# One late modulation sum per scan step, six among the intra-chunk matrices and four in the second branch

## The chip, the cores and the metric

The kernel runs on one core of a Trainium2 chip. A core has a matrix engine (TensorE, PE in the profile), a vector engine (VectorE, DVE), a scalar engine (ScalarE, ACT), a general engine (GpSimd, POOL) and a synchronising engine (SyncE, SP), which here issues the transfers between the chip's memory and the core's. Each engine runs its own instructions in order and waits on semaphores for the others. The metric is the time of one execution of the whole program in microseconds of the device, as a median of runs.

## What is computed

One layer of a hybrid backbone over 512 latent tokens (width 1024) and 256 context tokens: a modulated norm, one wide input projection, two mixers, a gated sum, an output projection, a second modulated norm and an MLP.

```
sh1, sc1, gt1, sh2, sc2, gt2 = split(silu(c) @ w_ada + b_ada, 6)
h  = rms_norm(x, g_norm1) * (1 + sc1) + sh1                  # hc likewise, for the context
aq, ak, av, dq, dk, dv, dz, da, db, ga, gd = split_cols(h @ w_in)
y_attn = window_ctx_attention(rope(norm(q)), rope(norm(k)), v, context k and v, sink)
o_d    = gated delta rule in both directions (chunks of 64), context state first, then latent
y = sigmoid(ga) * (y_attn @ w_br_attn) + sigmoid(gd) * ((rms_norm(o_d) * silu(dz)) @ w_br_dn)
x = x + gt1 * (y @ w_out)
x = x + gt2 * (relu(modulate(x, sh2, sc2) @ w_mlp1) ** 2 @ w_mlp2)
```

In the delta rule each chunk needs a triangular inverse, the matrix `intra = decay * (q k^T)` and, over the chunks, a scan that carries the state:

```
u = uv - w @ S;   o = q_dec @ S + intra @ u;   S = exp(g_last) * S + k_tail^T @ u
```

Of the modulation vector, the first two parts (`sh1`, `sc1`) are needed at the start. The other four (`gt1`, `sh2`, `sc2`, `gt2`) are needed only after the mixers; in this kernel they are the "late" part.

## The kernel before

The kernel is written in a tile framework: the program says what to compute and which buffers to use, and a scheduler orders the instructions of each engine by their dependences and their place in the program. So where a call stands in the code decides roughly, but not exactly, where its instructions run.

Activations lie transposed, with channels on the 128 partitions and the 512 tokens along the row. Every large product is a 128x512 matmul in three parts (high times high, high times low, low times high, `mm3`, L313 to L315), since each operand is split into a high and a low part: ScalarE copies the high part (L259 for weights, L184 for activations) and VectorE subtracts it for the low part (L262, L185). Weights come through a ring of four raw buffers of 512 KB (`wr`, L250) and two split ones (`wh`, `wl`).

**The fill.** Between the small matmuls of the delta rule (32 to 64 rows) PE runs large products of other work: the first branch's projection (`br_a`, 96 products) and the gate tiles (`gate_tiles`, 24 products for each tile, L1004, then an activation that L148 issues). `run_fill(n)` takes the next `n` of these 432 products. The table `FILL` says how many go where: 144 in the context scan, `FILL[1]` for each of the two `combine` calls, `FILL[2]` for each of the two intra-chunk calls, and three numbers (8, 7, 3) for the three phases of each latent scan step. What is left then runs after the scan. `combine` multiplies the halves of the inverse in two bursts of small matmuls (L854/L855 and L864/L865); between them ScalarE evicts the first result (L856) and `CPAUSE` products run.

**The intra-chunk matrices.** For each of two groups, `half_products` computes q k^T in two halves (L754), VectorE multiplies by the decay (L1245, L1246), and then for each of two halves of the partitions ScalarE copies blocks (L1252 twice, L1253, L1254), 32x512 each.

**The scan.** A step of `chain_step` runs for both directions in three phases: L1119 (state times key and query), VectorE's L1123 and L1124 (decay and difference), L1131 (times the inverse), L1137 and ScalarE's L1141 and L1143, then L1152/L1156 (state and output), L1168 (new state) and L1175 or L1178/L1180 (output). The last three set off the next step.

**The late sums.** `late_mod` computes the late modulation on VectorE. Each of the 32 sums loads 512 KB of `w_ada` into a slot of the same ring (`wa`, tag `wr`) and runs one instruction of 128x1024 with an accumulator (L1070); after each eighth, L1073 adds the bias. `run_late(n)` runs the next `n`, up to 24; the last eight run in the MLP's first part. Before, two of the three phases of each latent scan step take one (16 in all), and the output projection takes the other eight.

**After the scan.** The norm of the scan's output (L1178 to L1182, table loads on ScalarE, L1285), transposes on PE (L1290), the last gate tiles, then the second branch: eight tiles of 12 products (L1312's `mm3`), each evicted by L1314, added by L1316 and split by L184/L185 into `Y`. The output projection (`residual`, L1336) reads all eight `Y`.

Of the kernel before, what the change touches and what calls it, by code (L numbers as in the profile page):

```python
# [11 lines left out]
AF = mybir.ActivationFunctionType  # L12
# [3 lines left out]

NU = 167
NWR, NWS = 4, 2
FILL = 144, 28, 36, (8, 7, 3)
INV = 2, 12, 18, 0  # L20
QTS = 7, 5, 4, 7, 3, 6, 10, 7
CO = 1
# [4 lines left out]
WARM = 3, 6, 4, 4  # L27
NONES = 16
AHEAD = 2
LATE = 1  # L30
HPAUSE = 2
FPAUSE, CPAUSE = 12, 12
NPL = ()
WEARLY = 0
ND1 = 3
# [10 lines left out]
HC = CH // 2  # L46
# [53 lines left out]
def tile_layer(ctx: ExitStack, tc: tile.TileContext, I: dict, out: bass.AP, dbg=None):  # L100
# [995 lines left out]
    eGs = const.tile([P, 2, NM], F32, name="eGs")  # L1096
    for r in range(2):
        A.activation(eGs[64 * r:64 * r + 64], eG[64 * (1 - r):64 * (1 - r) + 64], AF.Copy)
    oss = small([P, NCL, 4], "oss", bufs=1)
    hv = lambda ap: ap.rearrange("p (q v) -> p q v", q=4)  # L1100
    state = [None, None]
# [134 lines left out]
    for g in range(2):  # L1236
        ms = slice(16 * g, 16 * g + 16)
        es = slice(512 * g, 512 * g + 512)
        run_fill(FILL[2] - FPAUSE)
        qq_ = bank(2)  # L1240
        qD, qO = diag_off(qq_)
        for _ in half_products(qq_, 1 + g, qT):
            run_fill(FPAUSE)
        for d in range(2):
            V.tensor_tensor(ia[d][:, ms, :HC], v3(ED[d][:, es]), qD, op=ALU.mult)  # L1245
        V.tensor_tensor(v3(EO[:, es]), v3(EO[:, es]), qO, op=ALU.mult)  # L1246
        qq_.free()
        eo = v3(EO[:, es])
        for a in range(2):
            lo, hi = quad(a, 0), quad(a, 1)  # L1250
            for d in range(2):
                A.activation(ia[d][hi, ms, HC:], ia[d][hi, ms, :HC], AF.Copy)  # L1252
            A.activation(ia[0][lo, ms, HC:], eo[lo], AF.Copy)  # L1253
            A.activation(ia[1][hi, ms, :HC], eo[hi], AF.Copy)  # L1254
            G.memset(ia[0][hi, ms, :HC], 0.0)
            G.memset(ia[1][lo, ms, HC:], 0.0)
# [6 lines left out]
    ot = ot_.ap.rearrange("p (c q v) -> p c q v", c=NCL, q=4)  # L1263
    for n, _ in enumerate(steps(range(NCC, NC_))):
        run_fill(FILL[3][n % 3])
        if n % 3:
            run_late(LATE)
    for _ in fill:
        pass
    for b in kT + qT + KTM[1:] + VTM[1:] + XA[1] + IA + zb + Sb[0] + Sb[1]:  # L1270
# [37 lines left out]
    Y = [alloc(1024) for _ in range(8)]  # L1308
    for ct in range(8):
        w = wnext()  # L1310
        pd = bank()
        mm3(pd.ap, w, [(r32(b[:, :512]), r32(b[:, 512:])) for b in yd])  # L1312
        g = gdt[ct].ap
        V.scalar_tensor_tensor(g, g, 1.0, pd.ap, op0=ALU.add, op1=ALU.mult)  # L1314
        pd.free()
        V.tensor_tensor(g, g, gat[ct].ap, op=ALU.add)  # L1316
        split(g, Y[ct][:, :512], Y[ct][:, 512:])
# [235 lines left out]
```

## Time and profile before

| | |
|---|---|
| runs | 928.25 us median of three (928.17 to 930.97) |
| profiled execution | 923.26 us, its span 921.5 us |
| granted TensorE clock, mean | 0.996 |
| PE busy | 886.7 us (96%) |
| DVE busy | 596.6 us (65%) |
| ACT busy | 447.6 us (49%) |
| late sums (L1070) | 32, 38.9 us of VectorE |
| intra-chunk stage, 360 to 401 us | PE busy 36.89 of 41.00 us |
| latent scan, 401 to 474 us | PE busy 68.46 of 73.00 us |

A row of a group names the line, the engine, the operation, what it writes and reads, the count, the busy time, the mean of one in nanoseconds, and the idle time before it with its releaser. A row of a wait names the line that waited and the one that released it. A row of the timeline has the start and the duration in microseconds, and in brackets the idle time before.

### The profile page before, as it was taken

To read this page: it belongs to the slowest core of one execution; us is meant where nothing else is said; L and a number is where in the kernel's file an instruction comes from. 1 tells how busy PE (TensorE), PEld (TensorE's weight loads), DVE (VectorE), ACT (ScalarE), POOL (GpSimd) and SP (SyncE) were. 2 spreads that over 40 slices of the span, in tenths; PEclk is the share of its full clock that TensorE was granted. 3 is DMA by queue.
4 is the path that set the end of the run, shared out by engine and by line. 5 is a ranking of instruction groups with operands and counts; after the bars stand their busy time and mean duration, and the time that the engine had idled before them with its cause. 6 is when DMAs were issued, how large, how long until landed. Compare 5 with 4: busy or idle time off the path is not lost.

```text
span 921.5 us, 16859 instructions
## 1 busy us (share of the span) xinstructions
PE 886.7 (96%) x7082; PEld 709.2 (77%) x7082; DVE 596.6 (65%) x1021; ACT 447.6 (49%) x829; POOL 12.0 (1%) x26
## 2 busy tenths in 40 slices
PE   8999998999899999989999999999999999999998
PEld 5668767867677687767778889888888888888886
DVE  3588899997687898358865977961554235324511
ACT  5577653257568787475554434560353025213400
POOL 0000000000000002000000000000000000000000
PEclk9999999999999999999999999999999999999999
DMA  9650112110000232236424673660443224322111
GB/s 355 255 197 1 47 47 68 50 49 19 24 13 23 58 109 78 92 109 189 142 81 149 193 245 114 212 243 23 160 137 115 69 69 138 100 69 83 46 46 46
DMA packets 28443, 98.24 MB, mean 107 GB/s; under 512 B 3536, under 2 KB 4176, under 8 KB 27344
## 3 DMA queue, kind: packets, MB, share of 16 engines
q1 hardware_dynamic: 28368, 97.18, 33.0%
q8 instruction: 55, 0.90, 0.4%
q14 instruction: 20, 0.16, 0.1%
HBM read 95.07 MB, written 2.10 MB: 105 GB/s over the span
## 4 chain that ended last, share of the span: by engine, by line
PE 45%; DVE 3%; DMA 3%; ACT 1%; issue 1%; ACTq 0%
PE banks L313 14%; PE banks L314 14%; PE banks L315 14%; PE banks L1004 3%; DMA wa<-in_wada 2%; DVE m L1070 1%; DVE wl L262 1%; DMA wr<-in_wm 0%; ACT wh L259 0%; DVE m L1168 0%; ACT m L1166 0%; PE banks L1131 0%; PE banks L1290 0%; PE banks L1156 0%; ACT m L148 0%
## 5 line engine op out<-in xcount | busy, mean ns | idle before, releaser
L313 PE MATMUL banks<-m,m 128*128 128x512 f32 (+1 forms) x600 | 223.4, 377 | 2.8 <-DVE m L620 1.9
L314 PE MATMUL banks<-m,m 128*128 128x512 f32 (+1 forms) x600 | 224.5, 376 | 0.1
L315 PE MATMUL banks<-m,m 128*128 128x512 f32 (+1 forms) x600 | 224.4, 376 | 0.0
L259 ACT ACTIVATE m<-wr 128x1024 fp32r<-128x1024 f32 x68 | 72.1, 1060 | 157.0 <-PE banks L314 79.7
L313 PEld LDWEIGHTS banks<-m,m 128*128 128x128 f32 x600 | 111.8, 188 | 25.6 <-ACT m L319 2.5
L314 PEld LDWEIGHTS banks<-m,m 128*128 128x128 f32 x600 | 112.5, 188 | 22.2 <-DVE m L320 1.5
L315 PEld LDWEIGHTS banks<-m,m 128*128 128x128 f32 x600 | 112.5, 188 | 21.4 <-issue 1.2
L262 DVE TENSOR_TENSOR m<-wr,m 128x1024 fp32r<-128x1024 f32 x68 | 83.1, 1224 | 69.9 <-PE banks L314 34.2
L1004 PE MATMUL banks<-m,wh 128*128 128x512 f32 x320 | 104.1, 402 | 2.6 <-ACT m L148 2.5
L313 PE MATMUL banks<-m,wh 128*128 128x512 f32 (+1 forms) x280 | 104.0, 372 | 2.5 <-DVE m L595 1.0
L315 PE MATMUL banks<-m,wl 128*128 128x512 f32 (+1 forms) x280 | 101.6, 365 | 3.4 <-DVE wl L262 3.4
L314 PE MATMUL banks<-m,wh 128*128 128x512 f32 (+1 forms) x280 | 102.4, 366 | 0.0
L1437 DVE SCALAR_TENSOR_TENSOR m<-banks,modT,m 128x512 f32<-128x512 f32 x32 | 24.0, 750 | 101.0 <-PE banks L315 101.0
L262 DVE TENSOR_TENSOR wl<-wr,wh 128x1024 fp32r<-128x1024 f32 (+1 forms) x58 | 62.1, 1071 | 29.7 <-ACT wh L259 29.3
L259 ACT ACTIVATE wh<-wr 128x1024 fp32r<-128x1024 f32 (+1 forms) x58 | 54.5, 940 | 40.1 <-PE banks L314 17.8
L1004 PEld LDWEIGHTS banks<-m,wh 128*128 128x128 f32 x320 | 59.1, 188 | 15.6 <-ACT m L148 2.9
L1004 PE MATMUL banks<-m,wl 128*128 128x512 f32 x160 | 65.4, 409 | 0.0
L315 PEld LDWEIGHTS banks<-m,wl 128*128 128x128 f32 x280 | 53.3, 192 | 11.9 <-DVE wl L262 4.0
L313 PEld LDWEIGHTS banks<-m,wh 128*128 128x128 f32 x280 | 53.5, 191 | 11.2 <-DVE m L595 1.3
L184 ACT ACTIVATE m<-m 128x512 fp32r<-128x512 f32 (+1 forms) x56 | 35.2, 631 | 54.9 <-DVE m L1420 21.5
L314 PEld LDWEIGHTS banks<-m,wh 128*128 128x128 f32 x280 | 53.4, 191 | 8.1 <-issue 1.0
L185 DVE TENSOR_TENSOR m<-m,m 128x512 fp32r<-128x512 f32 (+1 forms) x56 | 38.3, 688 | 18.8 <-ACT m L184 18.3
(237 smaller groups left out, 1266.5 us busy)
## 6 DMA issues: line engine op xcount, KB each, us to landing
wr<-in_wm SPq DMA_DIRECT2D x64, 512.0 KB, 3.6
wr<-in_win SPq DMA_DIRECT2D x38, 512.0 KB, 3.6
wa<-in_wada SPq DMA_DIRECT2D x32, 512.0 KB, 3.9
m<-in_wada SPq DMA_DIRECT2D x8, 1024.0 KB, 12.2
m<-in_xT SPq DMA_DIRECT2D x8, 512.0 KB, 5.8
wr<-in_wbr SPq DMA_DIRECT2D x16, 256.0 KB, 2.6
wr<-in_wout SPq DMA_DIRECT2D x8, 512.0 KB, 4.5
out<-m SPq DMA_DIRECT2D x8, 256.0 KB, 2.0
```

The lines of the kernel that those rows point to most:

```text
L184: A.activation(r32(hi), src, AF.Copy)
L185: (eng or V).tensor_tensor(r32(lo), src, hi, op=ALU.subtract)
L259: h = A.activation(r32(hi), raw, AF.Copy)
L262: V.tensor_tensor(r32(lo), raw, hi, op=ALU.subtract)
L313: PE.matmul(acc, w[0][:, k, :], xhi, start=(start and i == 0), stop=False)
L314: PE.matmul(acc, w[0][:, k, :], xlo, start=False, stop=False)
L315: PE.matmul(acc, w[1][:, k, :], xhi, start=False, stop=(stop and i == n - 1))
L1004: PE.matmul(acc.ap, w[x][:, k, :], hx[k][y], start=(k == p == 0), stop=(k == KT - 1 and p == 2))
L1070: V.scalar_tensor_tensor(t.ap, wa, 0.5, scr.ap, op0=ALU.mult, op1=ALU.mult, accum_out=modT[:, grp, j:j + 1])
L1437: V.scalar_tensor_tensor(xn_[ct], acc.ap, modT[:, 3, ct:ct + 1], xn_[ct], op0=ALU.mult, op1=ALU.add)
```

## The change

Five places differ. (1) `FILL[1]` goes from 28 to 36 and `CPAUSE` from 12 to 16: each `combine` has 20 and 16 products where it had 16 and 12. (2) A new `run_both` runs fill products and after each twelfth (`LATE`) one late sum; the intra-chunk groups use it, so that 72 products take six sums. (3) A scan step takes one late sum, in its last phase, where it took two. (4) Every second tile of the second branch takes one, four in all; the output projection's `run_late(2)` finds six left. (5) The eight copies of L1252 go from ScalarE to VectorE (`tensor_copy`).

```diff
-FILL = 144, 28, 36, (8, 7, 3)
+FILL = 144, 36, 36, (8, 7, 3)
...
-LATE = 1
+LATE = 12
...
-FPAUSE, CPAUSE = 12, 12
+FPAUSE, CPAUSE = 12, 16
...
+    def run_both(n):
+
+        for _ in range(n):
+            next(fill, None)
+            both[0] += 1
+            if both[0] % LATE == 0:
+                run_late(1)
+
+    both = [0]
...
-        run_fill(FILL[2] - FPAUSE)
+        run_both(FILL[2] - FPAUSE)
...
         for _ in half_products(qq_, 1 + g, qT):
-            run_fill(FPAUSE)
+            run_both(FPAUSE)
...
-                A.activation(ia[d][hi, ms, HC:], ia[d][hi, ms, :HC], AF.Copy)
+                V.tensor_copy(ia[d][hi, ms, HC:], ia[d][hi, ms, :HC])
...
         run_fill(FILL[3][n % 3])
-        if n % 3:
-            run_late(LATE)
+        if n % 3 == 2:
+            run_late(1)
...
     for ct in range(8):
         w = wnext()
+        run_late(ct % 2)
         pd = bank()
```

The line numbers of the changed program are 9 higher from the scan on (L1123 is L1132, L1124 is L1133, L1131 is L1140, L1252 is L1261, L1245 is L1254, L1290 is L1299) and 10 higher from the second branch on (L1314 is L1324, L1336 is L1346).

Three places in the order of instructions. First, ScalarE from the second group of the intra-chunk matrices to the first latent scan step (`wh` are high parts of weights, L148 a gate's activation, the numbered `m` are work buffers). Before:

```order
L259 ACTIVATE wh_4004<-wr_4002 128x1024
L1252 ACTIVATE m_3869<-m_3869 32x16x32
L1252 ACTIVATE m_3870<-m_3870 32x16x32
L1253 ACTIVATE m_3869<-m_759 32x16x32
L1254 ACTIVATE m_3870<-m_759 32x16x32
L1252 ACTIVATE m_3869<-m_3869 32x16x32
L1252 ACTIVATE m_3870<-m_3870 32x16x32
L1253 ACTIVATE m_3869<-m_759 32x16x32
L1254 ACTIVATE m_3870<-m_759 32x16x32
L148 ACTIVATE m_3999<-banks 128x512
```

Now, the rows from the same stretch:

```order
L259 ACTIVATE wh_3965<-wr_3963 128x1024
L148 ACTIVATE m_3960<-banks 128x512
L1262 ACTIVATE m_3885<-m_759 32x16x32 x2
L1263 ACTIVATE m_3886<-m_759 32x16x32 x2
L148 ACTIVATE m_4048<-banks 128x512
L259 ACTIVATE wh_4053<-wr_4051 128x1024
L1175 ACTIVATE m_4281<-m_2825,egl 128x64 x4
```

The eight copies of L1252 have left ScalarE, and the gate's L148 stands behind four copies instead of eight. They are on VectorE now, in the stretch ahead of the first latent scan step's L1132 and L1133:

```order
L262 TENSOR_TENSOR wl_4213<-wr_4210,wh_4212 128x1024
L1254 TENSOR_TENSOR m_3885<-m_757,banks 128x16x32
L1254 TENSOR_TENSOR m_3886<-m_758,banks 128x16x32
L1255 TENSOR_TENSOR m_759<-m_759,banks 128x512
L1261 COPY m_3885<-m_3885 32x16x32
L1261 COPY m_3886<-m_3886 32x16x32
L1261 COPY m_3885<-m_3885 32x16x32
L1261 COPY m_3886<-m_3886 32x16x32
L1132 TENSOR_TENSOR m_4185<-banks,eg 128x256
L1132 TENSOR_TENSOR m_4204<-banks,eg 128x256
L1133 SCALAR_TENSOR_TENSOR m_4185<-m_3144,m_4185 128x256
```

Before, that step's first L1123 and L1124 stood ahead of the second group's two L1245 and with no copy in front; now both directions' L1132 stand behind the whole second group.

Second, VectorE in one latent scan step (`eg` holds decays). Before:

```order
L1175 TENSOR_TENSOR m_4128<-m_4510,banks 128x256
L1070 SCALAR_TENSOR_TENSOR m_4679,modT<-wa_4677,m_3489 128x1024
L1123 TENSOR_TENSOR m_4596<-banks,eg 128x256
L1073 TENSOR_TENSOR modT<-modT,c_prm 128x8
L1070 SCALAR_TENSOR_TENSOR m_4824,modT<-wa_4822,m_3489 128x1024
L1124 SCALAR_TENSOR_TENSOR m_4596<-m_3144,m_4596 128x256
L1123 TENSOR_TENSOR m_4615<-banks,eg 128x256
```

Now:

```order
L1184 TENSOR_TENSOR m_4168<-m_4402,banks 128x256
L1070 SCALAR_TENSOR_TENSOR m_4617,modT<-wa_4615,m_3489 128x1024
L1132 TENSOR_TENSOR m_4485<-banks,eg 128x256
L1133 SCALAR_TENSOR_TENSOR m_4485<-m_3144,m_4485 128x256
L1132 TENSOR_TENSOR m_4504<-banks,eg 128x256
L1133 SCALAR_TENSOR_TENSOR m_4504<-m_3217,m_4504 128x256
```

The late sum between L1123 and L1124 is gone; the one ahead of them is left.

Third, VectorE at the end of the second branch, up to the output projection's first eviction. Before:

```order
L1316 TENSOR_TENSOR m_5457<-m_5457,m_3197 128x512
L262 TENSOR_TENSOR wl_5656<-wr_5653,wh_5655 128x1024
L185 TENSOR_TENSOR m_5497<-m_5457,m_5497 128x512
L1314 SCALAR_TENSOR_TENSOR m_5489<-m_5489,banks 128x512
L262 TENSOR_TENSOR wl_5686<-wr_5683,wh_5685 128x1024
L1316 TENSOR_TENSOR m_5489<-m_5489,m_3260 128x512
L1070 SCALAR_TENSOR_TENSOR m_5715,modT<-wa_5713,m_3489 128x1024
L185 TENSOR_TENSOR m_5498<-m_5489,m_5498 128x512
```

Now:

```order
L1326 TENSOR_TENSOR m_5448<-m_5448,m_3197 128x512
L1070 SCALAR_TENSOR_TENSOR m_5665,modT<-wa_5663,m_3489 128x1024
L185 TENSOR_TENSOR m_5488<-m_5448,m_5488 128x512
L1324 SCALAR_TENSOR_TENSOR m_5480<-m_5480,banks 128x512
L262 TENSOR_TENSOR wl_5694<-wr_5691,wh_5693 128x1024
L1326 TENSOR_TENSOR m_5480<-m_5480,m_3260 128x512
L1070 SCALAR_TENSOR_TENSOR m_5723,modT<-wa_5721,m_3489 128x1024
L185 TENSOR_TENSOR m_5489<-m_5480,m_5489 128x512
```

A late sum more stands among the last two tiles' evictions; two others stand at the second and the fifth tile, and one ahead of the first.

## The prediction

> **What bounds the kernel now.** I read the busy table first, then windows cut at the stages that the change touches (columns: stretch, its length, busy us and instructions of PE, PEld, DVE, ACT, POOL; granted clock, DMA share, GB/s).
>
> ```profile
> PE 886.7 (96%) x7082; PEld 709.2 (77%) x7082; DVE 596.6 (65%) x1021; ACT 447.6 (49%) x829; POOL 12.0 (1%) x26
> ```
>
> ```profile
> 360.00:401.00 41.00, 36.89 (x953) 29.34 (x952) 18.49 (x25) 26.66 (x48) 6.21 (x12) 1.00 0.30 89
> 401.00:474.00 73.00, 68.46 (x1324) 52.09 (x1323) 58.08 (x128) 43.06 (x147) 0.00 (x0) 1.00 0.48 145
> 474.00:497.00 23.00, 23.00 (x108) 18.53 (x107) 12.23 (x18) 10.54 (x17) 0.00 (x0) 1.00 0.32 103
> 497.00:520.00 23.00, 23.00 (x100) 18.48 (x99) 18.59 (x29) 11.99 (x18) 0.00 (x0) 1.00 0.52 161
> ```
>
> PE sets the end. The change neither adds nor removes a matmul, and the clock is 1.00 in all four stretches, so it can only win PE's idle time or add to it. That time is 41.00−36.89 = 4.1 us in the intra-chunk stage, 73.00−68.46 = 4.5 us in the latent scan, and none in the scan's tail (474–497) or the second branch (497–520). From the last row a product takes 23.00/100 = 0.23 us. The waits of PE from 360 to 480 us say who ends the idle time (total, times, longest):
>
> ```profile
> PE banks L1004 <- ACT m L148: 2.5, 1, 2.5
> PE banks L1131 <- DVE m L1124: 1.9, 2, 1.1
> PE banks L865 <- issue: 1.1, 1, 1.1
> PE banks L1119 <- DVE m L1168: 1.0, 2, 0.7
> PE banks L1152 <- DVE m L1137: 0.9, 1, 0.9
> PE banks L864 <- ACT m L856: 0.2, 1, 0.2
> ...
> ```
>
> So about 8 us can be won at all, and two stages without any idle time get new work on VectorE or lose cover. These are the terms.
>
> **Combine (L864, L865).** `FILL` and `CPAUSE` put 16 products instead of 12 between its halves and 20 ahead of them instead of 16. Four more products are 0.9 us, more than the 0.2 us for which L864 waits for L856: gain 0.2. The 1.1 us at L865 end with nothing that the profile shows. They come inside the second half's burst of 64 matmuls of 32 rows, so I read them as the engine's instruction supply falling behind in it; four more products straight ahead of that burst give the supply time. Bounds: 0, if the stall belongs to the burst alone, and 1.1. I take 0.8, since it comes in one of the two combines and not in the other, which makes it a matter of the spacing.
>
> **Half products and the first scan step.** ScalarE in the order that it runs, then PE and VectorE (start, duration):
>
> ```profile
> 390.11 1.15 ACT L1252 ACTIVATE m<-m 32x512 f32<-32x512 f32 x2
> ...
> 395.04 0.60 ACT L148 ACTIVATE m<-banks 128x512 f32<-128x512 f32 x1
> ```
>
> ```profile
> 395.69 0.73 PE L1004 MATMUL banks<-m,wh 128*128 128x512 f32 x2 [2.54 <-ACT m L148]
> ```
>
> ```profile
> 388.16 1.28 DVE L1245 TENSOR_TENSOR m<-m,banks 128x512 f32<-128x512 f32 x2 [4.00 <-PE banks L754]
> ...
> 391.26 0.42 DVE L1123 TENSOR_TENSOR m<-banks,eg 128x256 f32<-128x256 f32 x1
> ```
>
> The gate's activation L148 stands behind eight copies on ScalarE (four of L1252, two of L1253, two of L1254; from 390.11 to 395.04), and the bank it must empty is the one that the next gate tile needs. The change takes all of L1252's eight copies off ScalarE and puts L148 behind four copies only. Four copies of 1.15/2 = 0.58 us are 2.3 us, almost the whole 2.54 us, and the gate tile meets it at another place in its count: I take this wait to be gone.
>
> In its place VectorE gets the copies. In the changed order the second half products and the first scan products run together on PE, then come 13 products, then L1140, which needs the changed program's L1132 and L1133. Ahead of those stand, on VectorE, two L1254 (1.28), one L1255 (about 0.65), four copies, and L1132 and L1133 twice each (4 × 0.42, less overlap about 1.4); a weight split L262 may still be in front. The trace of before has no such copy on VectorE. The nearest rows bound it from both sides:
>
> ```profile
> L389 DVE CAST maskb<-m 128x256 bf16<-128x256 f32 x1 | 0.3, 284 | 0.0
> ```
>
> ```profile
> L185 DVE TENSOR_TENSOR m<-m,m 128x512 fp32r<-128x512 f32 x7 | 4.8, 688 | 0.9 <-ACT m L184 0.7
> L262 DVE TENSOR_TENSOR wl<-wr,wh 128x512 fp32r<-128x512 f32 x7 | 4.8, 685 | 4.9 <-ACT wh L259 4.9
> L1316 DVE TENSOR_TENSOR m<-m,m 128x512 f32<-128x512 f32 x7 | 4.8, 684 | 0.0
> L1314 DVE SCALAR_TENSOR_TENSOR m<-m,banks 128x512 f32<-128x512 f32 x7 | 4.8, 684 | 3.1 <-PE banks L315 3.1
> ```
>
> A one-source cast of half the width takes 0.28 us, a two-source instruction of the same width 0.69 us. I take 0.5, between them, since a one-source row exists and the width is twice its. Then the chain is 1.3+0.65+4×0.5+1.4 = 5.3 us, against 13×0.23 = 3.0 us of products and some 0.8 us for which the first scan products run after the half products: a new wait of 1.5 us, from 0.7 (copies at 0.28) to 2.3 (at 0.69), and up to 2.4 us more if both L262 get in front. Gain here: 2.5+0.6 (the rest of this stage's idle time, which I give half) −1.5 = about 1.6, from 0 to 2.5.
>
> [...]
>
> **The scan.** Six steps, each cut from one L1131 to the second next; then what stands in the chain where it is late:
>
> ```profile
> 413.89:422.01 8.12, 8.11 (x179) 6.21 (x178) 6.51 (x16) 4.75 (x20) 0.00 (x0) 1.00 0.46 133
> 422.01:431.86 9.85, 8.62 (x178) 6.41 (x179) 8.85 (x20) 5.50 (x20) 0.00 (x0) 1.00 0.77 220
> ...
> 451.24:459.04 7.80, 7.80 (x178) 6.02 (x178) 6.42 (x17) 2.35 (x8) 0.00 (x0) 1.00 0.38 126
> 459.04:469.47 10.43, 8.74 (x180) 6.59 (x179) 8.08 (x20) 6.94 (x26) 0.00 (x0) 1.00 0.37 103
> sum 55.58, PE 51.25 PEld 38.82 DVE 47.05 ACT 31.80 POOL 0.00; mean PE 8.54 PEld 6.47 DVE 7.84 ACT 5.30 POOL 0.00
> ```
>
> ```profile
> 429.83 0.42 DVE L1123 TENSOR_TENSOR m<-banks,eg 128x256 f32<-128x256 f32 x1
> ...
> 430.24 1.22 DVE L1070 SCALAR_TENSOR_TENSOR m<-wa,m 128x1024 f32<-128x1024 f32 x1
> ...
> 431.38 0.42 DVE L1124 SCALAR_TENSOR_TENSOR m<-m,m 128x256 f32<-128x256 f32 x1
> ```
>
> ```profile
> 448.64 1.22 DVE L262 TENSOR_TENSOR wl<-wr,wh 128x1024 fp32r<-128x1024 f32 x1
> ...
> 451.24 1.15 PE L1131 MATMUL banks<-m,m 64*64 64x64 f32 x32 [1.09 <-DVE m L1124]
> ```
>
> The same matmuls take 7.80 and 8.12 us where VectorE has 6.4 to 6.5 us of work, and 9.85 and 10.43 where it has 8 to 9. At 430.24 a late sum of 1.22 us sits between L1123 and L1124, that is, inside the chain on which the next L1131 waits. The change takes 16 late sums to 8; in the changed order five stand ahead of a step's first L1132, where VectorE waits for PE anyway, but in the last two steps one still stands between the second L1132 and its L1133. A step with a weight split in the chain (448.64, 1.22 us as well) stays long. So: six steps at 7.8 to 8.1 would be 48 us, 7.6 less than 55.58; two of them I leave 1.5 us long for L262 and L626, and 1.1 in all for the last two late sums and small waits: 7.6−3.0−1.1, gain 3.5. Upper bound 5.5 (one long step left); lower bound 2.0, the waits by name that hang on a late sum alone (0.8 of the 1.9 at L1131, the 1.0 at L1119, and 0.2 of the rest).
>
> **The switch.** In the changed order one run of products more is cut in two (13 and 2 of them between bursts of scan products), which is one change of matmul size and back:
>
> ```profile
> 414.97 0.50 PE L1004 MATMUL banks<-m,wh 128*128 128x512 f32 x1
> 415.31 0.39 PE L1004 MATMUL banks<-m,wl 128*128 128x512 f32 x1
> ```
>
> After a burst the next product follows at 0.34 us instead of 0.23, the first is 0.1 longer, and entering costs about as much: loss 0.3 (0.1 to 0.5).
>
> **The scan's tail.** The 16 products that were left for it now run earlier, so 25×0.23 = 5.8 us follow the last scan products instead of 39×0.23 = 9.0. Under them lies the normalisation:
>
> ```profile
> 475.15 0.74 DVE L1182 TENSOR_REDUCE oss<-m 128x4 f32<-128x256 f32 x2 [0.21 <-ACT m L1181]
> ```
>
> ```profile
> 481.47 2.36 DVE L1285 TENSOR_TENSOR m<-m,oss 128x1024 f32<-128x1024 f32 x2 [1.21 <-ACT oss L148]
> ```
>
> ```profile
> 482.76 1.09 PE L1290 MATMUL banks<-c_ident,m 128*128 128x128 f32 x8
> ```
>
> ```profile
> 479.51 1.28 ACT L144 ACT_TABLE_LOAD   x1
> ```
>
> From L1182's end at 475.9 the chain needs the table (1.28), two small activations (about 0.6) and the first half of L1285 (1.2): 479.0 if nothing stands ahead of it, where PE's cover ends at about 473.5+5.8 = 479.3. Before, it started at 479.51 because a weight copy and a gate activation were ahead on ScalarE; one of them still is (1.1 us). Loss 0.8, from 0 to 1.5.
>
> **Second branch.** Four late sums come into a stage where PE has no idle time. Per tile VectorE has L1314, L262, L1316 and L185, 4×0.685 = 2.74 us, against 12×0.23 = 2.76 on PE; the stage has 23.00−18.59 = 4.4 us free, and the four sums are 4×1.22 = 4.9. One runs ahead of the first tile. The other three (3.7) stand against the free time that is left once the first tile's start is passed, about 1.9 (half of L1314's 3.1 and of L185's 0.9), and this:
>
> ```profile
> 523.48 0.68 DVE L185 TENSOR_TENSOR m<-m,m 128x512 fp32r<-128x512 f32 x1
> ```
>
> ```profile
> 524.99 0.40 PE L314 MATMUL banks<-m,wh 128*128 128x512 f32 x1
> ```
>
> Y's last tile is ready at 524.16 and wanted from about 524.8, a slack of 0.6. 3.7−1.9−0.6 = 1.2 us: that is my loss at the first out-projection tile, the next in line after L185; bounds 0 (all free time can be used) and 2.5. The out projection then has six late sums instead of eight, which I count at nothing: PE has no named wait there. One MLP late sum moves ahead of the normalisation's L318, ahead of a wait of VectorE for ScalarE: nothing, at most 1.
>
> **Sum.** Gains 0.2+0.8+1.6+3.5 = 6.1 (2.2 to 9.3), losses 0.3+0.8+1.2 = 2.3 (0.1 to 5.5, with the MLP's). Net −3.8: the profiled execution of 923.26 us (span 921.5) would take about 919.5 and its span 917.7. The runs' median is 928.25, 5 us above that execution; I carry the difference over: 924.4 us.
>
> **Rivals.** (a) The waits only move: L262 and L626 keep the scan's chain late, so that it gains 2.0, and the new wait at L1140 eats the first step's gain. 2.2−2.3 is 0 us: 928.2, or 926.5 with the 1.1 us at L865. For it: steps are long wherever VectorE has 8 us or more, and L262 is as long as a late sum. Against it: the step at 413.89 had three late sums and was 8.12, so position matters more than load.
> (b) Slower: VectorE becomes the bound of the second branch. If free time there can't be used, since L1314 must wait for each tile's last product, L185 of tile 7 comes 3.7−0.6 = 3.1 us late, and each L262 behind a late sum adds its share, so that weights come late too: 4 to 5 us. With the tail's 1.5 and gains of 3 that is 931. It decides from where late sums exceed the usable free time by over 3 us. Against it: the free time in the rows is spread over the tiles, 0.5 us in most.
> (c) Weights come late: late sums take slots of the four-deep ring of weight buffers, now also in the intra-chunk stage, where DMA is busy at 0.30 only. If L259 waits there, PE loses some 1 to 2 us per event; one event makes it 926. The stage's low share speaks against it.
> (d) The change does less than it says: the scheduler moves late sums back into the scan's chains. In the changed order no step has two, so the 16 are 8, and only the last two are in a chain; nothing more for it.
>
> **How the numbers follow.** Forecast 0.54, (a) 0.22, (b) 0.11, (c) 0.12, (d) 0.01. A measurement tells 0.3%, 2.8 us, from no change: below 925.5 is faster. The forecast's own range, 921 to 926.5, lies below that in six of seven; (a) lies within 0.3% but for one case in ten; (c) is faster in one case of three; (b) is slower in four cases of five. Faster 0.53, same 0.37, slower 0.10. The range reaches from 920, most gains and few losses, to 928.8, which takes in (a) and (c).
>
> **What would show it.** Right: no wait of L1004 on L148 near the half products, a wait of about 1.5 us at L1140 on L1133 in its place; scan steps of 7.8 to 8.2 us but for two to four; PE waits of 0.5 to 1.5 us at the first L1299 and at the first out-projection tile on L185. Wrong: scan steps still above 9 us with one late sum each (then L262, not L1070, was the load), a wait at L185 of 3 us or more, or named DMA waits ahead of L259.

## The result, and the profile after

The changed kernel took 921.91 us (median of six executions, 919.27 to 922.56), the kernel before 928.21 us (median of six on the same chip, 924.26 to 930.97): a ratio of 0.9937, interval 0.9909 to 0.9964, or 5.8 us of 928 (the two medians differ by 6.3). That is faster by more than 0.3%, inside the predicted range (920.0 to 928.8) and 2.5 us below the predicted 924.4. A second time, with twelve executions, it gave 0.9939 (0.9921 to 0.9957). Ratios here leave out three slow executions of the kernel before (1090, 1232 and 2200 us), which came in later comparisons.

The two profiled executions differ far less: the spans are 921.5 and 920.4 us. The page of the changed kernel and the waits of PE from 360 to 580 us (total, times, longest):

```profile
PE 885.5 (96%) x7082; PEld 708.7 (77%) x7082; DVE 600.8 (65%) x1029; ACT 442.7 (48%) x821; POOL 12.9 (1%) x26
```

```profile
PE banks L1140 <- DVE m L1133: 6.2, 5, 3.9
PE banks L754 <- DVE m L1255: 1.2, 1, 1.2
PE banks L1004 <- issue: 1.1, 1, 1.1
PE banks L1004 <- ACT m L148: 0.5, 1, 0.5
PE banks L313 <- ACT m L319: 0.3, 1, 0.3
PE banks L865 <- issue: 0.3, 1, 0.3
```

The wait of 2.5 us for L148 has become one of 3.9 us at the first L1140 (the rest of the 6.2 us are four waits of 0.3 to 0.7 us in the scan), and a new one of 1.2 us stands at the half products. On the other side, L1119, L1152 and L864 no longer wait, and from 480 to 560 us no wait is left at all. Windows cut at the stages (columns as before; the last three numbers are clock, DMA share and GB/s):

```profile
360.00:410.00 50.00, 45.67 (x977) 35.82 (x975) 29.38 (x42) 25.11 (x47) 6.37 (x12) 1.00 0.46 150
410.00:416.00 6.00, 4.51 (x100) 3.66 (x101) 3.76 (x10) 2.43 (x7) 0.70 (x1) 0.72 0.00 0
416.00:477.30 61.30, 57.84 (x1204) 44.38 (x1204) 44.77 (x104) 38.09 (x134) 0.00 (x0) 1.00 0.33 97
477.30:497.00 19.70, 19.66 (x108) 15.96 (x105) 12.81 (x19) 10.25 (x16) 0.00 (x0) 1.00 0.25 72
```

The second row is new: right behind the wait of 3.9 us PE's clock is granted at 0.72 on average over 6 us, which is what 3.4 us at half clock give (microsecond by microsecond from 411 to 415 us: 0.57, 0.50, 0.50, 0.72). VectorE at that place:

```profile
402.49 1.22 DVE L262 TENSOR_TENSOR wl<-wr,wh 128x1024 fp32r<-128x1024 f32 x1 [0.39 <-ACT wh L259]
405.35 1.23 DVE L262 TENSOR_TENSOR wl<-wr,wh 128x1024 fp32r<-128x1024 f32 x1 [1.64 <-ACT wh L259]
406.49 1.28 DVE L1254 TENSOR_TENSOR m<-m,banks 128x512 f32<-128x512 f32 x2
407.68 0.68 DVE L1255 TENSOR_TENSOR m<-m,banks 128x512 f32<-128x512 f32 x1
408.40 1.83 DVE L1261 COPY m<-m 32x512 f32<-32x512 f32 x4
410.26 0.76 DVE L1132 TENSOR_TENSOR m<-banks,eg 128x256 f32<-128x256 f32 x2
410.93 0.75 DVE L1133 SCALAR_TENSOR_TENSOR m<-m,m 128x256 f32<-128x256 f32 x2
```

```profile
411.49 1.97 PE L1140 MATMUL banks<-m,m 64*64 64x64 f32 x32 [3.88 <-DVE m L1133]
```

The four copies took 1.83 us, 0.46 each. But the half products were done at 403.3, and L1254, which needs nothing else, started only at 406.49: both L262 stood ahead of it in VectorE's queue, and the second waited 1.64 us for ScalarE. Those 3.2 us are most of the 3.88.

Where the time went, by landmarks that both programs share (start of the same matmul in each trace; a fill product counts 0.232 us, the median from one L1004 to the next in the trace of before, since the two programs have run different numbers of them at a landmark):

| stretch | before, us | after, us | products more in after | gain, us |
|---|---|---|---|---|
| last L1049 to the last L865 (combines) | 38.30 | 40.86 | 16 | 1.15 |
| to the first L1156 / L1165 (first scan step) | 32.24 | 34.90 | −2 | −3.1 |
| to the last L1156 / L1165 (scan) | 64.12 | 63.03 | 2 | 1.55 |
| to the first L1290 / L1299 (tail) | 9.46 | 6.27 | −14 | −0.05 |
| to the last L1004 | 13.75 | 13.23 | −2 | 0.05 |
| to the norm's L1363 / L1373 (second branch, output projection) | 67.98 | 66.39 | 0 | 1.6 |
| to the end | 357.0 | 357.0 | 0 | 0.05 |

This sums to some 1.2 us. The other 4 to 5 us of the medians are not in this pair of traces, and the first experiment was made for them.

### The profile page after: what moved, and what is told of

It reads as the page before. It is cut to its first block, busy times and chain, and to the rows that moved or that the text cites. A ratio compares the mean times of both kernels' runs of the same rounds, so it can differ in the third digit from the quotient of the medians.

```text
span 920.4 us, 16843 instructions
## 1 busy us (share of the span) xinstructions
PE 885.5 (96%) x7082; PEld 708.7 (77%) x7082; DVE 600.8 (65%) x1029; ACT 442.7 (48%) x821; POOL 12.9 (1%) x26
## 4 chain that ended last, share of the span: by engine, by line
PE 78%; DVE 11%; ACT 5%; DMA 3%; issue 2%; SPq 0%; DVEq 0%; ACTq 0%
PE banks L315 18%; PE banks L313 18%; PE banks L314 18%; PE banks L1004 8%; PE banks L1049 2%; DMA wa<-in_wada 2%; DVE wl L262 1%; PE banks L571 1%; PE banks L1140 1%; PE banks L577 1%; PE banks L639 1%; PE banks L1161 1%; PE banks L578 1%; DVE m L1070 1%; DMA m<-in_xT 1%
## 5 line engine op out<-in xcount | busy, mean ns | idle before, releaser
L313 PE MATMUL banks<-m,m 128*128 128x512 f32 (+1 forms) x600 | 223.5, 377 | 2.8 <-DVE m L620 1.9
L314 PE MATMUL banks<-m,m 128*128 128x512 f32 (+1 forms) x600 | 224.5, 376 | 0.1
L315 PE MATMUL banks<-m,m 128*128 128x512 f32 (+1 forms) x600 | 224.5, 376 | 0.0
L259 ACT ACTIVATE m<-wr 128x1024 fp32r<-128x1024 f32 x68 | 71.7, 1059 | 151.6 <-PE banks L314 79.0
L313 PEld LDWEIGHTS banks<-m,m 128*128 128x128 f32 x600 | 111.9, 188 | 25.4 <-ACT m L319 2.5
L314 PEld LDWEIGHTS banks<-m,m 128*128 128x128 f32 x600 | 112.5, 188 | 22.1 <-DVE m L320 1.5
L315 PEld LDWEIGHTS banks<-m,m 128*128 128x128 f32 x600 | 112.5, 188 | 21.3 <-issue 1.2
L262 DVE TENSOR_TENSOR m<-wr,m 128x1024 fp32r<-128x1024 f32 x68 | 83.1, 1224 | 66.9 <-PE banks L314 34.2
L1004 PE MATMUL banks<-m,wh 128*128 128x512 f32 x320 | 105.0, 406 | 1.6 <-issue 1.1
L313 PE MATMUL banks<-m,wh 128*128 128x512 f32 (+1 forms) x280 | 103.8, 372 | 1.5 <-DVE m L595 1.0
L315 PE MATMUL banks<-m,wl 128*128 128x512 f32 (+1 forms) x280 | 101.6, 365 | 3.1 <-DVE wl L262 3.1
L314 PE MATMUL banks<-m,wh 128*128 128x512 f32 (+1 forms) x280 | 102.6, 367 | 0.0
L259 ACT ACTIVATE wh<-wr 128x1024 fp32r<-128x1024 f32 (+1 forms) x58 | 54.5, 940 | 46.6 <-PE banks L314 19.5
L262 DVE TENSOR_TENSOR wl<-wr,wh 128x1024 fp32r<-128x1024 f32 (+1 forms) x58 | 62.2, 1073 | 18.8 <-ACT wh L259 18.8
L1004 PEld LDWEIGHTS banks<-m,wh 128*128 128x128 f32 x320 | 58.2, 189 | 14.4 <-issue 0.9
L1004 PE MATMUL banks<-m,wl 128*128 128x512 f32 x160 | 64.5, 403 | 0.0
L315 PEld LDWEIGHTS banks<-m,wl 128*128 128x128 f32 x280 | 53.3, 192 | 11.7 <-DVE wl L262 3.9
L313 PEld LDWEIGHTS banks<-m,wh 128*128 128x128 f32 x280 | 53.6, 192 | 10.1 <-DVE m L595 1.3
L314 PEld LDWEIGHTS banks<-m,wh 128*128 128x128 f32 x280 | 53.5, 191 | 8.2 <-issue 1.0
L1070 DVE SCALAR_TENSOR_TENSOR m<-wa,m 128x1024 f32<-128x1024 f32 x32 | 38.9, 1222 | 19.4 <-DMA wa<-in_wada 14.4
```

The lines of the kernel that those rows point to most:

```text
L259: h = A.activation(r32(hi), raw, AF.Copy)
L262: V.tensor_tensor(r32(lo), raw, hi, op=ALU.subtract)
L313: PE.matmul(acc, w[0][:, k, :], xhi, start=(start and i == 0), stop=False)
L314: PE.matmul(acc, w[0][:, k, :], xlo, start=False, stop=False)
L315: PE.matmul(acc, w[1][:, k, :], xhi, start=False, stop=(stop and i == n - 1))
L1004: PE.matmul(acc.ap, w[x][:, k, :], hx[k][y], start=(k == p == 0), stop=(k == KT - 1 and p == 2))
```

## The experiments

### The kernel before and the changed kernel, once more

No edit in either.

> The kernel before, unchanged, to see how its executions spread. Theory: the profiled execution of before (923.26 us) was one of its quick ones; its other executions lose up to 7 us to stretches in which the granted clock is low, so their spans rise as their mean clock falls, and the median stays near 928. Rival: the slow executions have the same mean clock, about 0.996, and a longer wait somewhere; then span and clock are not related.

> The changed kernel unchanged, beside the kernel before on one chip, for its size and its spread. Theory: 5 us below before (ratio 0.994 to 0.995), with the wait of 3 to 4 us at the first L1140 and a stretch of half clock behind it in the profile again. Rival: the 6 us measured at first are chance of the early runs, and the difference of the two profiled spans, about 1 us, is the truth: ratio above 0.997.

The kernel before, run as if it were a change, took 928.22 us (twelve executions, 924.33 to 930.66) beside 926.47 (35 executions): 1.0017, interval 1.0000 to 1.0034. That is what no change can look like here: differences below 0.2% say nothing. The mean granted clock of an execution and its time go together: of 45 executions of before, the eleven at 0.996 averaged 925.2 us, fifteen at 0.994 averaged 926.6 and eight at 0.991 averaged 929.4. The first theory of e1 held. The profiled execution of before, 923.26 us at 0.996, was one of the quickest of all. A profile of the same kernel at 0.992 shows what a slower execution has (first the quick trace of before, then e1's; same stretches):

```profile
392.00:394.00 2.00, 1.14 (x50) 0.91 (x39) 1.42 (x3) 1.96 (x4) 0.52 (x1) 1.00 0.78 199
394.00:400.00 6.00, 4.31 (x19) 3.52 (x20) 3.10 (x6) 5.83 (x11) 1.04 (x2) 1.00 0.13 37
```

```profile
392.00:394.00 2.00, 0.04 (x1) 0.00 (x0) 0.40 (x1) 1.93 (x5) 0.52 (x1) 0.97 0.56 205
394.00:400.00 6.00, 5.44 (x13) 4.33 (x14) 3.10 (x6) 5.85 (x12) 1.04 (x2) 0.50 0.26 81
400.00:402.00 2.00, 2.00 (x9) 1.60 (x8) 0.00 (x0) 1.00 (x5) 0.00 (x0) 0.82 0.09 31
```

Both have the wait of 2.5 us of L1004 for L148. In the second trace the clock is then granted at 0.50 for six us, and 13 products run there instead of 19: between the last L754 and the first L1156 it loses 2.6 us against the quick trace. So the 2.5 us of idle time of before cost up to 5.1 us, and which it is differs from execution to execution. In the profiles of this study the half clock followed in every one where PE had waited 3.3 us or more at this place (five of five), in two of three profiles with 2.5 or 2.6 us, and in none with 1.7 us or less (six, at 1.00 from 385 to 420 us). Later in the program it followed a wait of 6.7 us (in `e8_scan_only`, below, at 0.95 on average from 520 to 560 us), and did not follow waits of 3.2 us (`e3_nointra`) and 2.45 us (`e10_fill28`), both at 1.00 over the same stretch. What decides it after a wait of 2.5 us no run shows.

How many of before's executions have the half clock at this place is not shown. The mean clock does not say where it was low, and there are other such stretches: the quick trace itself has 0.91 from 140 to 160 us and 0.91 from 240 to 260 us, the changed kernel's has 0.83 and 1.00 there.

The changed kernel gave 921.18 us (918.06 to 924.31) beside before (926.98): 0.9939, and its profile has the wait of 3.9 us and the low clock behind it again:

```profile
410.00:415.00 5.00, 3.70 (x98) 3.06 (x98) 3.31 (x10) 2.05 (x7) 0.50 (x1) 0.77 0.00 0
415.00:420.00 5.00, 5.00 (x99) 3.72 (x93) 3.89 (x11) 4.65 (x17) 0.00 (x0) 0.89 0.31 81
```

The rival, that 1 us is the truth, fell.

The profiles of e1 and e5 have the half clock in both kernels, so they are a second pair for the table above, and one nearer to the medians. In it the combines gain 1.4 us, the first scan step 1.05, the scan 1.05, the tail −0.1, the last L1004 0.05, the second branch and output projection 1.6, and the rest 1.05: 6.1 us. (The spans, 924.5 and 920.2 us, differ by 4.3 us only, since e5's trace is 1.8 us later at the last L1049.) The first step comes out at −3.1 us in one pair and +1.05 in the other for two reasons: the half clock of before costs 2.6 us there in e1's trace, and in e5's the changed kernel's own half clock reaches over the first L1165, at 413.3 us, into the scan. So the first step and the scan are best taken together: −1.55 us against the quick trace, +2.1 us with the half clock in both.

### The intra-chunk late sums, out and elsewhere

```diff
-LATE = 12
+LATE = 1000
```

> The changed kernel without late sums among the intra-chunk matrices; the six run later, in the output projection and straight ahead of the second norm. Theory: the 1.15 us for which L754 waits for L1255, which stood behind a late sum whose transfer was late, are gone, and nothing else changes in that stage, the wait of 3.9 us included; the later places lose some of it: 921 to 923. Rival: the late sums in that stage are also what sets the first scan step late; then its wait falls below 2 us.

The time was 923.33 us (0.9965, 0.9949 to 0.9980). The waits of PE from 355 to 580 us:

```profile
PE banks L1140 <- DVE m L1133: 3.5, 4, 1.7
PE banks L313 <- ACT wh L259: 3.4, 2, 3.2
...
PE banks L313 <- DVE m L1346: 0.6, 1, 0.6
```

The theory, that the wait of 3.9 us would stay, failed, and the rival was right on the first step: the wait there fell from 3.9 to 1.74 us, with no half clock behind it, and L754 no longer waits. VectorE's queue explains it (the second L262, and what follows):

```profile
402.89 1.23 DVE L262 TENSOR_TENSOR wl<-wr,wh 128x1024 fp32r<-128x1024 f32 x1 [3.23 <-ACT wh L259]
404.03 1.28 DVE L1254 TENSOR_TENSOR m<-m,banks 128x512 f32<-128x512 f32 x2
```

The second half products were done at 402.9 here, and L1254 came 1.1 us behind them, not 3.2. In the changed kernel a late sum, whose 512 KB were late, stood ahead of the first group's eviction:

```profile
395.11 1.23 DVE L1070 SCALAR_TENSOR_TENSOR m<-wa,m 128x1024 f32<-128x1024 f32 x1 [3.21 <-DMA wa<-in_wada]
396.26 1.28 DVE L1254 TENSOR_TENSOR m<-m,banks 128x512 f32<-128x512 f32 x2
```

That moved L754 (the wait of 1.2 us), then the gate's activation, and with them ScalarE's weight copy: the L259 in front of the second L262 started at 404.3 us, 2.1 us behind the second half products' start, and in this run at 401.8, ahead of theirs. At the last L1004 this kernel was 4.5 us ahead of the changed one (both from the last L1049 on). It lost 4.2 us of that by the norm, since ten sums in the output projection and two in front of the norm held up the weights (the wait of 3.2 us for L259). So the six sums cost where they are, and cost as much at the end. The next kernel puts them where VectorE and DMA had room, behind the scan (from 477.3 to 497 us VectorE is busy for 12.81 of 19.70 us and the DMA share is 0.25 in the changed kernel):

```diff
-LATE = 12
+LATE = 1000
...
-    for _ in gate_tiles(gates[12 + NGD:]):
-        pass
+    for n, _ in enumerate(gate_tiles(gates[12 + NGD:])):
+        if n % 12 == 6:
+            run_late(1)
```

> The changed kernel with the six late sums of the intra-chunk matrices run among the last gate products behind the scan (474 to 497 us), where VectorE had half its time free. Theory: the first scan step waits about 1.7 us as without them there (not 3.9), no half clock behind it, no wait of L754 for L1255, and the second branch and output projection stay as in the changed kernel: 4 us below it, about 917.5. Rival: the six take the weights' ring slots there as well, and weights are late in the tail or the second branch by 3 us or more: 921 or above.

919.07 us (six executions, 918.09 to 920.62), 0.9921 (0.9893 to 0.9949), about 2 us below the changed kernel where 4 were expected. Its first L1140 waits 1.7 us, the clock stays at 1.00 from 385 to 560 us, and nothing waits for weights. At the place itself the gain came in full: from the last L865 to the last L1156 this trace is 4.0 us shorter than e5's. From the norm on it is 1.0 us longer, with a wait of 1.1 us of L313 for L319 where 0.3 stood before: two late sums now stand ahead of the norm's first L318 on VectorE, where the changed kernel has one. The other 1 us of the missing 2 is not assigned.

### The first scan step: copies and cover

The copies alone went back to ScalarE in the changed kernel:

```diff
-                V.tensor_copy(ia[d][hi, ms, HC:], ia[d][hi, ms, :HC])
+                A.activation(ia[d][hi, ms, HC:], ia[d][hi, ms, :HC], AF.Copy)
```

> The changed kernel with the eight copies back on ScalarE. Theory (VectorE's queue at the first latent scan step): VectorE's chain ahead of the first L1140 is 1.8 us shorter, so the wait of 3.9 us there falls to about 2 to 3, with fewer products ahead of it in the order; time 920 to 921.5. Rival (ScalarE's queue): the gate's activation stands behind eight copies again and PE waits 2 us or more for L148; time 923 or more.

922.25 us, 0.9953 (0.9939 to 0.9967): between the theory's time and the rival's, and not told apart from the changed kernel. The wait at L1140 is 3.4 us and no wait for L148 came back (0.5). VectorE's chain is 1.8 us shorter, but the order has eight products ahead of L1140 instead of 13 (1.2 us less cover), and both L262 still stand in front. So neither the copies nor ScalarE's queue are the main thing here any more; it is what stands ahead of the evictions.

Then 16 products of the second group were put behind its evictions:

```diff
-        run_both(FILL[2] - FPAUSE)
+        run_both(FILL[2] - FPAUSE - 16 * g)
...
         qq_.free()
+        run_both(16 * g)
```

> The changed kernel with 16 of the second group's products run behind its evictions instead of ahead of its half products. Theory: 16 products (3.7 us) cover VectorE's chain of evictions and copies ahead of the first scan step, the wait of 3.9 us at the first L1140 and the stretch of halved clock behind it are gone: 4 to 5 us less, some 0.7 back for two more changes of matmul size: 917.5 to 918.5. Rival: VectorE's total work between the half products and the first scan step is the bound, so the wait only moves: within 1 us of the changed kernel.

923.21 us, 0.9961 (0.9943 to 0.9979). The wait at the first L1140 was gone (the longest at L1140 is 0.7 us), but the wait only moved, as the rival said, and the half clock with it; the time is 1.3 to 2 us above the changed kernel. The second group's half products come 16 products earlier and wait for the first group's eviction, which stands behind a late sum and its transfer:

```profile
PE banks L754 <- DVE m L1255: 3.3, 1, 3.3
PE banks L1140 <- DVE m L1133: 2.9, 5, 0.7
```

```profile
394.72 1.23 DVE L1070 SCALAR_TENSOR_TENSOR m<-wa,m 128x1024 f32<-128x1024 f32 x1 [2.89 <-DMA wa<-in_wada]
...
395.87 1.28 DVE L1254 TENSOR_TENSOR m<-m,banks 128x512 f32<-128x512 f32 x2
```

VectorE idled 2.89 us for the late sum's transfer with the eviction ready behind it. This is the plainest row of the study: a late sum that has not landed holds the whole queue.

### Parts of the change alone

The copies alone, in the kernel before:

```diff
-                A.activation(ia[d][hi, ms, HC:], ia[d][hi, ms, :HC], AF.Copy)
+                V.tensor_copy(ia[d][hi, ms, HC:], ia[d][hi, ms, :HC])
```

> The kernel before with only the eight copies moved to VectorE. Theory: the 2.5 us wait of L1004 for L148 goes, and with it the stretch of half clock behind it in most executions; in its place comes a wait of at most 1.5 us at L1131 or L754: 2 to 4 us below before. Rival: VectorE's queue is the bound there, and PE waits as long for L1124: no change.

925.08 us, 0.9985 (0.9967 to 1.0003), 1.9 us by the medians, just below the theory's 2 to 4; the interval reaches no change. The wait of 2.5 us is gone (0.6 us left in two waits for L148), and the clock stays at 1.00 at this place. From the last L1049 to the last L1004 this trace is only 0.3 us shorter than the quick trace of before, and 3.4 us shorter than e1's: by these traces, what the copies win is mostly the half clock that no longer follows.

One sum per scan step, in the kernel before:

```diff
-        if n % 3:
-            run_late(LATE)
+        if n % 3 == 2:
+            run_late(1)
```

> The kernel before with only one late sum per scan step; the eight others run in the output projection and ahead of the second norm. Theory: from the first L1156 to the last one the scan is 3 to 3.5 us shorter, with waits at L1131 of 2 us or less; at the end of the output projection, where six more late sums stand ahead of the norm, 4 us or more are lost, so the time is 0 to 3 us above before. Rival: the scan's steps are set by the weight splits L262 and not by late sums; then the scan is at most 1.5 us shorter.

932.06 us, 1.0059 (1.0041 to 1.0078). From the first to the last L1156 the scan takes 61.84 us instead of 64.12, 2.3 us less: between the theory's 3 and the rival's 1.5. But the eight sums that the scan gave up had nowhere to go, and PE waits for the eviction behind them at the end of the output projection:

```profile
PE banks L313 <- DVE m L1336: 7.0, 2, 6.7
```

So the gain in the scan is real, and worth nothing without places for the sums.

Back to the old `FILL` and `CPAUSE`, the rest as in the change:

```diff
-FILL = 144, 36, 36, (8, 7, 3)
+FILL = 144, 28, 36, (8, 7, 3)
...
-FPAUSE, CPAUSE = 12, 16
+FPAUSE, CPAUSE = 12, 12
```

> The changed kernel with FILL and CPAUSE as before (16 and 12 products around each combine). Theory: the two waits of the combine come back (0.2 at L864, about 0.9 at L865 without a cause in the profile) and the wait of that kind in the scan goes, since it is one shortage of instructions that turns up at one place or the other; net within 1 us from that. The order interleaves the first scan products with the half products as in the kernel before, which changes the first L1140 wait too. Rival: the spacing truly removes the stall, and without it 1 us or more is lost with nothing back.

928.54 us, 1.0015 (1.0004 to 1.0025): this edit, which I had costed at 1 us, undid the whole gain. From the profile: the combine waits came back (1.9 us at L865 with no cause shown, 0.2 at L864, and none of that kind in the scan). The first scan step was better (31.00 us from the last L865 to the first L1165, with as many products as the changed kernel has in 34.90 and, in e5's trace, in 33.33): its order interleaves the first scan products with the half products, and no half clock follows. And the second branch and output projection took 69.78 us instead of 66.39. What differs there is seen on SP's queue, in the issue of the input's 2 MB that the residual needs (first the changed kernel, then this one; L1336 is the line of this load here, and L1326 in the kernel before):

```profile
493.50 1.33 SPq L1336 DMA_DIRECT2D m<-in_xT  x3
...
499.75 0.42 SPq L1336 DMA_DIRECT2D m<-in_xT  x1
```

```profile
521.13 1.75 SPq L1336 DMA_DIRECT2D m<-in_xT  x4
522.93 0.74 SPq L250 DMA_DIRECT2D wr<-in_wout  x1
```

```profile
532.63 0.51 PE L313 MATMUL banks<-m,wh 128*128 128x512 f32 x1 [2.45 <-ACT wh L259]
...
533.89 0.50 PE L315 MATMUL banks<-m,wl 128*128 128x512 f32 x1 [0.52 <-DVE wl L262]
```

The buffers for these 2 MB are taken from space that others have left. Here the loads were issued 21 to 28 us later, they met the output projection's weights and late sums, and PE waited 2.5 and 0.5 us for a weight. That the late loads are the reason is argued from the queue's times; it was not tried by itself. Nor is it the old fill alone that makes them late: the kernel before, with the same fill, issued these loads from 491 to 494 us. From the norm to the end this kernel took 1.25 us longer as well, with no cause known. All this is 3.7 us of span; the medians differ by 6.6 or more, and the profiled execution was the quickest of the twelve, so some 3 us of this kernel's loss are not explained.

### The second branch

```diff
-        run_late(ct % 2)
```

> The changed kernel with no late sums in the second branch; the output projection takes ten instead of six. Theory (the four are free in the branch and cost in the output projection): the branch's end does not move, and the output projection waits again at L313 for the eviction L1346 or for weights, 1.5 us or more: 922.5 to 926. Rival (the prediction's term): VectorE is late at the end of the branch because of the four, and without them the time falls by about 1.2 us.

924.45 us, 0.9966 (0.9951 to 0.9981): 2.5 to 3.3 us above the changed kernel. The last L1004 does not move (0.2 us), and from there to the norm it takes 68.80 us instead of 66.39, with waits at L313 for an eviction (1.0 us), at L315 for L262 (0.8) and for L319 (1.0 in two). The theory held, and the prediction's term of 1.2 us for this place has the wrong sign: the four sums cost nothing in the branch, and save the 2.4 us that ten sums cost in the output projection.

### Better than both

Both last kernels have the six sums behind the scan; e11 also has the copies on ScalarE, e12 has eight products behind the second group's evictions (`8 * g` where e4 has `16 * g`).

> The six late sums behind the scan, and the eight copies back on ScalarE. Theory: VectorE's chain ahead of the first L1140 is 1.8 us shorter, the wait of 1.7 us there goes but for some tenths, ScalarE's copies are no longer in front of a gate's activation that PE wants: 0.5 to 1.5 us below the kernel with the six behind the scan (919.1). Rival: L1004 waits for L148 by 2 us or more again: 920 or above.

> The six late sums behind the scan, and eight of the second group's products behind its evictions instead of ahead of its half products. Theory: eight products more (1.9 us) cover the wait of 1.7 us at the first L1140; one more change of matmul size costs 0.35: about 1.3 us below 919.1. Rival: the wait only moves to the half products (L754 for L1255), whose cover shrinks by the same eight products: 919 or above.

e11 took 920.72 us (0.9926, 0.9910 to 0.9942), no better than e6. That is the rival's time, but not by its wait, which stayed at 0.5 us: the first L1140 waits 0.9 us or less, but L1165 now waits 1.1 us for ScalarE's L1150, behind the copies. e12 took 918.71 us (four executions, 917.68 to 919.55), 0.9909 (0.9893 to 0.9924), the lowest median of the study, 2.5 us below the changed one's 921.18 (whose ratio is 0.9939; the intervals just meet). The 1.3 us below e6 that were expected are not shown: the medians differ by 0.4 us, the intervals overlap, and from the last L1049 on the two traces take the same time within 0.2 us. Its waits of PE from 355 to 590 us:

```profile
PE banks L1140 <- DVE m L1133: 2.6, 4, 0.9
PE banks L1004 <- issue: 1.3, 1, 1.3
PE banks L313 <- ACT m L319: 1.1, 1, 1.1
PE banks L1004 <- ACT m L148: 0.5, 1, 0.5
```

No wait is longer than 1.3 us, L754 waits for nothing since no late sum stands before the evictions, and the clock stays at 1.00 from 385 to 560 us.

## Why the prediction was right, and where it was not

The sign and the range held, and the 5.8 us measured are half as much again as the 3.8 forecast. Two of the terms behind them did not hold, and their errors had opposite signs. Where two figures are given below, the first is from the table, against the quick trace of before, and the second from e1's and e5's traces.

**Combine: +1.0 predicted, +1.15 and +1.4 at the place, 0 in all.** The waits at L864 and L865 went nearly as costed. But the 1.1 us without a cause came back as 1.1 us at an L1004 in the scan (at 427 us). In all fourteen profiles 0.6 to 1.9 us of it stand at L865 (the five with the old fill) or in the scan (the nine with the new one), never at both in full. "A matter of the spacing" was the wrong reading: the spacing moved it. A count of PE's records (weight loads, matmuls, semaphore instructions, from 0 in the order of their starts) in the traces of before and after says more: the stall comes at record 6593 in the first (an L865 at 376.9 us) and at record 8129 in the second (an L1004 at 427.0 us), whose 0.3 us at L865 stand at its record 6593 as well. So in these two it hangs on a place in PE's own stream of instructions, whichever work stands there. Both pages list a queue of instruction transfers (q8, 55 packets, 0.90 MB); that this supply falls behind there, on which the prediction's 0.8 us rested, was my estimate, and no run shows it: no row names the releaser, and why the stall comes at one place or the other stays open.

**The first scan step: +1.6 predicted, −3.1 and +1.05 measured.** This is the step that failed, and the +1.05 does not save it: it is there because the kernel before lost 2.6 us to the half clock in e1's trace, which the prediction did not have. The wait that I foresaw at L1140 came, and its size was about right where the late sums of that stage are out (1.5 us predicted, 1.74 in e3, though there with one L262 in front of L1254). I had written that a weight split might be in front and would cost up to 2.4 us more; it was in front, and the late sums' transfers, which I had priced at nothing here, made it and L754 later: 3.9 and 1.2 us of waits instead of 1.74 and none, 3.3 us in all. The prediction's rival (c), at a chance of 0.12, is the nearest to this, but not what happened: its sign, L259 waiting for a weight, did not come. What waited for its transfer was the late sum itself, 3.2 us with the eviction ready behind it. Also, of the 1.6 us, the 0.6 for the rest of the stage's idle time was hardly there: 4.1 us less 2.5, 1.1 and 0.2 leave some 0.2. The copy was 0.46 us (four in 1.83 us; the median of the eight is 0.41), where I had taken 0.5.

**The clock: not in the prediction.** Every execution was taken to have the clock of the profiled one. Where the half clock follows the old wait of 2.5 us, that wait costs 2.6 us more, so removing it was worth up to 5 us instead of 2.5. That is how a change can lose 3.1 us at this place in one pair of traces and gain 1.05 in another.

**The scan: +3.5 predicted, +2.6 measured** (1.55 in the table and the 1.1 us that the stall without a cause took in it); alone, in e8, 2.3. The mechanism was right: the wait at L1119 is gone, and of the three steps that are left over 9 us one has a weight split and one a late sum between L1132 and L1133; the third has the stall. Its size was 0.9 us too large. The steps are not 7.8 to 8.2 us with two exceptions, as forecast, but 8.0 to 9.9. The change of matmul size and back (−0.3) was not measured by itself; in the trace of before, most bursts of the scan without a wait start 0.32 to 0.33 us after the last L1004 ahead of them, where two products follow each other at 0.23.

**The tail: −0.8 predicted, −0.05 and −0.1 measured.** PE is busy for 19.66 of 19.70 us behind the last scan products. The chain that I had let start at 475.9 follows the shorter cover without a gap, at the lower end of the bound.

**The second branch: −1.2 predicted, +1.6 measured for the branch and output projection.** VectorE was as full as I had said: counted from the last L1004, the last L185 ends 1.9 us later than before (at 526.67 instead of 524.16 us). But I had held fixed when it is wanted, and PE's order had moved: the first product that fits it (an L314 at 527.72 instead of 524.99 us) comes 2.1 us later too, with nine more products ahead of it, so no wait came. That this product is the one that needs it is read from the order; no row names it. And "no named wait" of PE in the output projection was false. The kernel before has these, at 557 and 550 us, behind the 480 us at which the prediction's list of waits ends:

```profile
PE banks L313 <- DVE m L1336: 0.9, 1, 0.9
PE banks L315 <- DVE wl L262: 0.3, 1, 0.3
```

With six sums instead of eight there, both are gone.

So the time came out near the forecast partly by luck. The first step, the scan and the change of matmul size were to give 4.8 us together and gave 2.1 even with the half clock in both traces; the second branch and output projection, which were to cost 1.2, gave 1.6; and the tail cost 0.7 less than forecast. Some 1 us from the norm on, in e1's and e5's traces alone, has no cause known.

## What to carry to other kernels

A long wait of PE can cost more than itself: price a wait of 2.5 us or more, by this kernel's figures, with the half clock that may follow (2.6 us more in e1's trace), and look at the granted clock behind it in more than one execution before a profile is taken for the kernel. Work that "needs only an idle engine" also needs its place in that engine's queue and its transfer to have landed; here a sum of 1.2 us that waited 2.9 us for its data held the evictions that PE wanted. And when deferred work is moved, find it a place before the gain is counted: the same eight sums were worth 2.3 us in the scan and cost 7 us at the output projection's end.

## What was not expected of the hardware

The wait of 2.5 us was followed by a granted clock of 0.50 in one execution of the kernel before and not in another (a difference of 2.6 us), and waits of 1.7 us at this place never were. The half clock lasted for about 3.4 us behind the changed kernel's wait and for twice that in e1's trace. A stall of 0.6 to 1.9 us on PE whose cause no row names moves from one place to another 50 us later when the number of products ahead changes, and stands at record 6593 of PE's stream in the trace of before and at record 8129, 1536 later, in the changed kernel's. The copy of 32x512 in 32-bit floats took 0.46 us on VectorE (four in 1.83) where ScalarE needed 0.58 to 0.62 (two in 1.15 us; 0.62 in the median of the eight).
